# A row-sum kernel: late waits alone on SyncE's store and end, and the last row split into 576 and 448 columns

## The chip, the cores and the metric

The kernel runs on one core of one Trainium2 chip. The metric is the device time in microseconds (us) of one execution. The profile's span (first to last instruction) is about 1.8 us shorter than the device time, and times "at 157.9 us" count from the span's start.

Besides the profile's views, the argument uses the trace's records: the start of every instruction, also those of a sequencer alone, and every increment of a semaphore. A load "lands" here when its semaphore gets the last of its 16 increments. VectorE "signals" when the semaphore of its last operation is incremented. Both are recorded to the nanosecond.

Some terms: SyncE issues the loads and stores here, VectorE and ScalarE compute. A semaphore is a counter that an engine or a transfer raises and that others wait for. A sequencer handles an engine's instructions in order (SPq and DVEq in the views are those of SyncE and VectorE). A nop computes nothing, but can be given waits. The drain and the closing barrier are the program's last steps. "issue" in a chain of waits is time in which the engine waited for nothing that the profile shows.

## The reference

```python
# x: (32, 512, 1024) float32, multiplier: 0.5
def reference(x, multiplier):
    return (np.sum(x, axis=-1) * multiplier).astype(np.float32)
```

This is 16384 row sums over 67 MB of input. Each of the 128 partitions takes 128 rows.

## The kernel before

The kernel loads blocks of 16 rows per partition into three buffers, all from SyncE. In each of the first seven blocks VectorE sums eight rows and ScalarE sums eight. The results of these seven blocks, 112 rows per partition that lie together in memory (the pitch of 112 rows below), leave in one early store. The last block comes in five loads, so that little work is left when the last bytes land. Its last row is split into two pieces of columns, summed by two VectorE operations, of which the second starts from the first's sum.

```python
    own = rows - B                                   # 112 rows per partition
    out_rows = out_flat[0 : P * own].rearrange("(p c) -> p c", p=P)
    # ... pools, and the loop over the first seven blocks ...

    def dve_span(t, r, lo, hi, dst, start=0.0):
        mid = (lo + hi) // 2
        nc.vector.tensor_tensor_reduce(              # (left half + right half) * mul, summed into dst
            out=t[:, r, lo:mid], in0=t[:, r, lo:mid], in1=t[:, r, mid:hi],
            scale=mul, scalar=start, op0=ADD, op1=ADD, accum_out=dst,
        )

    cut = 640
    pieces = [(0, 8), (8, 13), (13, 15)]             # rows of the last block: three loads
    # ...
    for lo, hi in ((0, cut), (cut, D)):              # the last row: two loads
        loads.append(nc.sync.dma_start(
            out=t[:, B - 1, lo:hi], in_=x_last[:, B - 1, lo:hi]))
    nc.sync.dma_start(out=out_rows, in_=res[:, 0:own])           # the early store
    on_act = {4, 5, 6, 7, 11, 12, 14}
    # ... rows 0 to 14: ScalarE those of on_act, VectorE the others ...
    dve_span(t, B - 1, 0, cut, part)
    dve_span(t, B - 1, cut, D, res[:, rows - 1 : rows], start=part)

    seen = nc.sync.nop()                             # waits for the last 8 loads and ScalarE's last row
    # ... its dependencies ...
    store = nc.sync.dma_start(out=out_last, in_=res[:, own:])    # the last store
    # ... ordered behind seen ...
```

When an instruction has more waits than it can carry, the compiler puts semaphore instructions, which only wait, in front of it. In the records such an instruction carries at most two waits, and a store carries one. A nop with waits is not seen itself: its waits show up on semaphore instructions. How these waits are dealt out is what the change is about.

Of the kernel before, what the change touches and what calls it, by code (L numbers as in the profile page):

```python
# [1 line left out]

# [4 lines left out]


@with_exitstack
def kernel(  # L10
    ctx: ExitStack,
    tc: tile.TileContext,
    x: bass.AP,
    multiplier: float,
    out: bass.AP,
):








    nc = tc.nc
    P = nc.NUM_PARTITIONS
    fp32 = mybir.dt.float32
    ADD = mybir.AluOpType.add

    x_flat = x.flatten_outer_dims()  # L30
    N, D = x_flat.shape
    rows = N // P
    out_flat = out.rearrange("b s -> (b s)")
    mul = float(multiplier)

    B = 16
    n_blocks = rows // B
    assert N == P * rows and rows == n_blocks * B
    own = rows - B
    x_rows = x_flat[0 : P * own, :].rearrange("(p c) d -> p c d", p=P)  # L40
    x_last = x_flat[P * own : N, :].rearrange("(p c) d -> p c d", p=P)
    out_rows = out_flat[0 : P * own].rearrange("(p c) -> p c", p=P)
    out_last = out_flat[P * own : N].rearrange("(p c) -> p c", p=P)

    x_pool = ctx.enter_context(tc.tile_pool(name="x", bufs=3))
    res_pool = ctx.enter_context(tc.tile_pool(name="res", bufs=1))
    sums = res_pool.tile([P, rows], fp32, name="sums")
    res = res_pool.tile([P, rows], fp32, name="res")
    part = res_pool.tile([P, 1], fp32, name="part")

    loads = []
    acts = []

    def act_row(t, r, col):
        acts.append(nc.scalar.activation(  # L55
            out=t[:, r, :],
            in_=t[:, r, :],
            func=mybir.ActivationFunctionType.Copy,
            scale=mul,
            accum_out=res[:, col : col + 1],  # L60
        ))

    def dve_span(t, r, lo, hi, dst, start=0.0):
        mid = (lo + hi) // 2
        nc.vector.tensor_tensor_reduce(  # L65
            out=t[:, r, lo:mid],
            in0=t[:, r, lo:mid],
            in1=t[:, r, mid:hi],
            scale=mul,
            scalar=start,  # L70
            op0=ADD,
            op1=ADD,
            accum_out=dst,
        )

    for b in range(n_blocks - 1):
        c0 = b * B
        t = x_pool.tile([P, B, D], fp32, name="xb")
        loads.append(nc.sync.dma_start(out=t, in_=x_rows[:, c0 : c0 + B, :]))  # L79
        h = B // 2  # L80
        nc.vector.reduce_sum(  # L81
            out=sums[:, c0 : c0 + h], in_=t[:, 0:h, :], axis=mybir.AxisListType.X
        )
        nc.vector.tensor_single_scalar(  # L84
            out=res[:, c0 : c0 + h],
            in_=sums[:, c0 : c0 + h],
            scalar=mul,
            op=mybir.AluOpType.mult,
        )
        for r in range(h, B):  # L90
            act_row(t, r, c0 + r)

    c0 = (n_blocks - 1) * B
    t = x_pool.tile([P, B, D], fp32, name="xb")
    cut = 640
    pieces = [(0, 8), (8, 13), (13, 15)]
    for lo, hi in pieces:
        loads.append(
            nc.sync.dma_start(  # L99
                out=t[:, lo:hi, :], in_=x_last[:, lo:hi, :]  # L100
            )
        )
    for lo, hi in ((0, cut), (cut, D)):
        loads.append(
            nc.sync.dma_start(
                out=t[:, B - 1, lo:hi], in_=x_last[:, B - 1, lo:hi]
            )
        )
    nc.sync.dma_start(out=out_rows, in_=res[:, 0:own])
    on_act = {4, 5, 6, 7, 11, 12, 14}  # L110
    for r in range(B - 1):
        if r in on_act:
            act_row(t, r, c0 + r)
        else:
            dve_span(t, r, 0, D, res[:, c0 + r : c0 + r + 1])
    dve_span(t, B - 1, 0, cut, part)
    dve_span(t, B - 1, cut, D, res[:, rows - 1 : rows], start=part)



    seen = nc.sync.nop()
    for i in loads[-8:] + acts[-1:]:
        tc.add_manual_dep(
            seen.ins,
            i.ins.name,
            mybir.DependencyInfo(mybir.DependencyClass.Sync, mybir.DependencyReason.DATA),
            reason="ends seen early",
        )
    store = nc.sync.dma_start(out=out_last, in_=res[:, own:])
    tc.add_manual_dep(  # L130
        store.ins,
        seen.ins.name,
        mybir.DependencyInfo(mybir.DependencyClass.NoSync, mybir.DependencyReason.SCHED_ONLY),
        reason="in this order",
    )

    def start_loads_at_entry(nc_):



        entry, *rest = nc_.main_func.blocks
        is_sp = lambda i: i.engine == mybir.EngineType.SP
        is_load = lambda i: type(i).__name__ == "InstDMACopy"
        for block in rest:
            body = list(block.instructions)
            own = [i for i in body if is_sp(i)]
            if not any(is_load(i) for i in own):
                continue
            lead = []
            for i in own:  # L150
                if not is_load(i) or i.sync_info.on_wait:
                    break
                lead.append(i)
            names = {i.name for i in lead}
            block.instructions = [i for i in body if i.name not in names]
            head = list(entry.instructions)
            at = next(
                k for k, i in enumerate(head) if is_sp(i) and type(i).__name__ == "InstDrain"
            )
            entry.instructions = head[:at] + lead + head[at:]  # L160
            return

    nc.at_finalize(start_loads_at_entry)


# [1 line left out]
_INS = ['x', 'multiplier']  # L167
_OUTS = [((32, 512), 'float32')]

_NUMBERS = {'multiplier': 0.5}  # L170


# [26 lines left out]
```

## Time and profile before

| | before |
|---|---|
| time, median of 3 runs | 162.62 us (162.53 to 162.68) |
| span of the profile | 160.83 us |
| last load lands | 157.888 us |
| last landing to the end of the span | 2.938 us |
| VectorE, ScalarE busy | 42%, 42% |

The page of the kernel before, its span, its memory traffic and the chain that ended last, in shares of the span:

```profile
span 160.8 us, 236 instructions
...
HBM read 67.11 MB, written 0.07 MB: 418 GB/s over the span
## 4 chain that ended last, share of the span: by engine, by line
DMA 86%; DVE 11%; SPq 1%; issue 0%; DVEq 0%
```

Input DMA is 86% of the chain; the 11% of VectorE are reductions whose end frees a buffer for the next load. The change touches none of this. What it can reach is the tail after the last landing. The timeline from there on gives start, duration, engine, line, operation and operands:

```profile
157.47 0.49 DVE L65 CUSTOM_DVE_ANT_0 xb<-xb 128x320 f32<-128x320 f32 x1
157.58 0.18 ACT L55 ACTIVATION_READ_ACCUMULATOR xb<-xb 128x1 f32 x1
157.89 0.08 DVE L65 DVE_READ_ACCUMULATOR2_ANT part<- 128x1 f32 x1
158.02 0.42 DVE L65 CUSTOM_DVE_ANT_0 xb<-xb,part 128x192 f32<-128x192 f32 x1
158.37 0.08 DVE L65 DVE_READ_ACCUMULATOR2_ANT res<- 128x1 f32 x1
158.60 0.34 SPq L129 DMA_DIRECT2D out_dram<-res  x1
```

The two CUSTOM_DVE lines are the two spans of the last row (320 and 192 output columns, half of the columns read). The store goes out at 158.60. The end of the chain of waits, in order of time (start, us, what), shows what the profile holds responsible:

```profile
109.71 47.74 DMA xb<-in_x_dram
157.45 0.02 issue
157.47 0.49 DVE xb L65
157.96 0.02 DVE part L65
157.98 0.04 issue
158.02 0.42 DVE xb L65
```

By this view the second span (158.02) followed the first one's sum (`part`, 157.98).

The same stretch in the records of SyncE's sequencer (start in us, duration in ns, what the instruction waits for; these are not lines of a view):

```
157.947    28  semaphore instruction   ScalarE, load of the 640 columns
158.477    28  semaphore instruction   VectorE's last span, an old load
158.537    28  semaphore instruction   two old loads
158.604   344  store                   ScalarE
160.029    28  semaphore instruction   the store's landing (160.012), the early store
160.094     7  drain                   VectorE
160.152     7  drain                   closing barrier
```

VectorE signals at 158.461. A semaphore instruction with nothing new to wait for stands between that and the store, and the store itself carries a wait that was met at 157.78.

### The profile page before, as it was taken

The page shows a single profiled execution, that of the slowest core. Times are in us where ns is not written, and L with a number is a line of the kernel's source. Part 1 is how long each engine was busy: PE and PEld are TensorE (multiplying, and loading weights), DVE is VectorE, ACT ScalarE, POOL GpSimd, SP SyncE. Part 2 cuts the span into 40 slices and gives each one's busy share as a digit, 9 for nine tenths or more (in the row PEclk, how much of TensorE's full clock was granted, in tenths as well). Part 3 has the DMA queues.
Part 4 walks back from the last instruction along what each step waited for, and adds up shares of the span by engine and source line. Part 5 has one row for each costly group of instructions (what it writes and reads, how often), then busy time and mean ns, then how long its engine had stood idle before and what let it go on. Part 6 is the DMA issues. An engine that isn't in the chain of part 4 may idle for free.

```text
span 160.8 us, 236 instructions
## 1 busy us (share of the span) xinstructions
DVE 68.1 (42%) x34; ACT 67.9 (42%) x127; POOL 0.2 (0%) x4
## 2 busy tenths in 40 slices
DVE  0000059600794009920199002990049700597453
ACT  3000059500793009910099002980039700596952
POOL 0000000000000000000000000000000000000000
DMA  7996996996996996996996996996996996998990
GB/s 261 522 522 261 522 522 261 522 522 261 522 522 261 522 522 261 522 522 261 522 524 261 522 505 277 522 505 277 522 505 277 522 489 293 408 489 381 413 390 23
DMA packets 2017, 67.18 MB, mean 418 GB/s; under 512 B 480, under 2 KB 608, under 8 KB 736
## 3 DMA queue, kind: packets, MB, share of 16 engines
q1 hardware_dynamic: 2016, 67.18, 97.3%
q14 instruction: 1, 0.01, 0.0%
HBM read 67.11 MB, written 0.07 MB: 418 GB/s over the span
## 4 chain that ended last, share of the span: by engine, by line
DMA 86%; DVE 11%; SPq 1%; issue 0%; DVEq 0%
DMA xb<-in_x_dram 86%; DVE sums L81 11%; SPq L99 1%; DVE xb L65 1%; SPq L79 0%; DVE part L65 0%; DVEq L194 0%
## 5 line engine op out<-in xcount | busy, mean ns | idle before, releaser
L55 ACT ACTIVATE xb<-xb 128x1024 f32<-128x1024 f32 x63 | 65.6, 1042 | 88.2 <-DMA xb<-in_x_dram 88.2
L81 DVE TENSOR_REDUCE sums<-xb 128x8 f32<-128x8192 f32 x7 | 60.8, 8686 | 85.0 <-DMA xb<-in_x_dram 85.0
L55 ACT ACTIVATION_READ_ACCUMULATOR xb<-xb 128x1 f32 x63 | 11.8, 187 | 0.0
L65 DVE CUSTOM_DVE_ANT_0 xb<-xb 128x512 f32<-128x512 f32 (+1 forms) x9 | 5.6, 667 | 5.1 <-DMA xb<-in_x_dram 4.9
L55 ACT ACT_TABLE_LOAD x1 | 1.3, 1283 | 1.7 <-PEq L180 1.7
L84 DVE TENSOR_SCALAR res<-sums 128x8 f32<-128x8 f32 x7 | 1.2, 171 | 0.2
L65 DVE DVE_READ_ACCUMULATOR2_ANT res<- 128x1 f32 x9 | 0.7, 83 | 0.0
L65 DVE CUSTOM_DVE_ANT_0 xb<-xb,part 128x192 f32<-128x192 f32 x1 | 0.4, 419 | 0.1
L180 POOL MEMSET const-bfloat16-1.0<- 128x1 bf16 x1 | 0.1, 101 | 0.0
L180 POOL MEMSET const-uint8-127<- 128x1 uint8 x1 | 0.1, 101 | 0.0
L180 POOL MEMSET const-float32-0.0<- 128x1 f32 x1 | 0.1, 98 | 0.2 <-issue 0.2
L180 POOL MEMSET const-float32-1.0<- 128x1 f32 x1 | 0.1, 98 | 0.0
L65 DVE DVE_READ_ACCUMULATOR2_ANT part<- 128x1 f32 x1 | 0.1, 83 | 0.0
## 6 DMA issues: line engine op xcount, KB each, us to landing
xb<-in_x_dram SPq DMA_DIRECT2D x1, 4096.0 KB, 39.6
xb<-in_x_dram SPq DMA_DIRECT2D x1, 2560.0 KB, 45.4
xb<-in_x_dram SPq DMA_DIRECT2D x1, 1024.0 KB, 47.4
xb<-in_x_dram SPq DMA_DIRECT2D x1, 320.0 KB, 47.7
xb<-in_x_dram SPq DMA_DIRECT2D x1, 192.0 KB, 47.7
xb<-in_x_dram SPq DMA_DIRECT2D x7, 49.6
out_dram<-res SPq DMA_DIRECT2D x1, 56.0 KB, 10.8
out_dram<-res SPq DMA_DIRECT2D x1, 8.0 KB, 1.4
```

The source lines that it names most:

```text
L55: acts.append(nc.scalar.activation(out=t[:, r, :], in_=t[:, r, :], func=mybir.ActivationFunctionType.Copy, scale=mul, accum_out=res[:, col ...
L65: nc.vector.tensor_tensor_reduce(out=t[:, r, lo:mid], in0=t[:, r, lo:mid], in1=t[:, r, mid:hi], scale=mul, scalar=start, op0=ADD, op1=ADD, ...
L81: nc.vector.reduce_sum(out=sums[:, c0 : c0 + h], in_=t[:, 0:h, :], axis=mybir.AxisListType.X)
L84: nc.vector.tensor_single_scalar(out=res[:, c0 : c0 + h], in_=sums[:, c0 : c0 + h], scalar=mul, op=mybir.AluOpType.mult,)
L99: nc.sync.dma_start(out=t[:, lo:hi, :], in_=x_last[:, lo:hi, :])
L180: nc = _bacc.Bacc("TRN2", target_bir_lowering=False, num_devices=1)
```

## The change

The intent is that each late event is awaited by the instruction that needs it, with every older wait passed before. ScalarE's dependency is taken off the store, as the nop in front waits for it. A second nop behind the store waits for what the end would otherwise wait for, while the store is in flight. The last row is cut at 576 columns instead of 640. The 112-row pitch of the loads and the early store is in both kernels and is no edit here.

```diff
-    cut = 640
+    cut = 576
...
-    nc.sync.dma_start(out=out_rows, in_=res[:, 0:own])
+    early = nc.sync.dma_start(out=out_rows, in_=res[:, 0:own])
...
-    dve_span(t, B - 1, cut, D, res[:, rows - 1 : rows], start=part)
+    final = dve_span(t, B - 1, cut, D, res[:, rows - 1 : rows], start=part)
...
-    seen = nc.sync.nop()
-    (its dependencies, written out)
+    seen = nop_after(nc.sync, loads[-8:] + acts[-1:], [])
     store = nc.sync.dma_start(out=out_last, in_=res[:, own:])
     (ordered behind seen)
+    for a in acts[-len(on_act) :]:
+        tc.declare_no_dep(store.ins, a.ins.name, reason="waited for by the nop in front")
+    nop_after(nc.sync, [early, final], [store])
```

`nop_after(engine, waits_for, follows)` makes a nop that waits for the ends of the first list and is ordered behind the second.

## The prediction

> **What bounds the kernel.** The input's DMA. The page gives 67.11 MB read at 418 GB/s over a 160.8 us span, VectorE and ScalarE busy 42% each. The chain of waits is input DMA and the VectorE work that frees buffers (97%) up to the last landing near 157.9 us; the change touches none of that: the same bytes, issues and buffers. The pitch of 112 rows is already in the kernel before (the store and loads use it), so that part of the title is no edit here. What is left is the tail, 157.4 to 160.8 us.
>
> **The tail before** (timeline from 156 us, and the records of SyncE's sequencer and semaphores):
> - The last row's 640 columns land at 157.45, its 384 columns at 157.89. VectorE starts the first span at 157.470, its result is signalled at 157.98; the second span starts at 158.022 and signals at 158.461. So the first span's compute, not the last landing, releases the second: over 0.05 us after it could have.
> - SyncE then passes two semaphore instructions at the store's line (158.477 and 158.537) and issues the store at 158.604: 0.143 us from the signal to the issue. Only the first carries something late (VectorE's end); the rest had been true for long or since 157.95.
> - The store lands 1.41 us later, at 160.012. Then one semaphore instruction (160.029), a drain (160.094), and the closing barriers to 160.826.
>
> **What the change does.**
> 1. *Store.* ScalarE's dependency is dropped from the store, since the nop ahead waits for it. That should leave VectorE's end as the wait carried by the store itself, with the stale waits passed in front of it by about 158.1. Two semaphore instructions, 0.060 and 0.067 us in the trace, leave the path: estimate -0.12 us.
> 2. *End.* The early store's and VectorE's waits go into a nop behind the store, under its 1.41 us flight. The drain waits for the store alone: one semaphore instruction, 0.065 us, leaves: estimate -0.06 us.
> 3. *Split 576/448.* The first piece should land about 0.08 us earlier (the last engine's bytes, 20 KB before, took 0.85 us; 18 KB now), the last unchanged. VectorE's operation costs 492 ns for 320 output columns and 419 for 192, so 0.57 ns each: 288 cost 474, 224 cost 437. The first span is signalled at about 157.88, the second starts at the last landing, about 157.97, and signals at 158.42: estimate -0.04 us.
>
> All three lie in series on the path; together -0.22 us. The Trainium skill ("Perfetto Trace Analysis", Identifying Dependency Chains) says that several waits may put EventSemaphore instructions before an instruction; this trace agrees (two at the store, one at the end). The store's flight stays[...].
>
> **Prediction:** 162.41 us, 8 in 10 between 162.25 and 162.57. Chances: faster by over 2% 0.01, within 2% 0.98, slower 0.01.
>
> **What the profile should show.** The store issues under 0.05 us after VectorE's last signal, with no semaphore instruction between (step 1); the drain follows the store's landing directly, under 0.03 us (step 2); the second span starts within 0.1 us of the last landing and the first is done by then (step 3). Span near 160.6 us; loads unchanged up to 157.9.
>
> **What would make it wrong.** The compiler places waits its own way and leaves a stale one behind the late one; SyncE is still passing old waits when VectorE ends; the last landing moves by more than the 0.2 us sought (runs of the kernel before already spread 0.15 us); the second nop delays the end.

## The result

| | before | after |
|---|---|---|
| time, median of 6 runs each | 162.61 us (162.53 to 162.73) | 162.44 us (162.34 to 162.51) |
| last load lands (one profile) | 157.888 us | 157.827 us |
| last landing to the end of the span | 2.938 us | 2.791 us |

A ratio in this document is the mean time of one kernel's fast runs over that of the other's in the same rounds, so it is not quite the ratio of the medians. Here it is 0.9989, with a 95% interval from 0.9976 to 1.0002: the same within 2%, as forecast, and inside the range. The timed runs alone do not quite show a gain. The trace shows one in the tail, because the stretch after the last landing repeats to within a few ns.

The page of the kernel after, the lines that answer to those above:

```profile
span 160.6 us, 236 instructions
...
HBM read 67.11 MB, written 0.07 MB: 418 GB/s over the span
## 4 chain that ended last, share of the span: by engine, by line
DMA 86%; DVE 11%; SPq 1%; issue 0%; DVEq 0%
```

The timeline of the tail:

```profile
157.33 0.46 DVE L78 CUSTOM_DVE_ANT_0 xb<-xb 128x288 f32<-128x288 f32 x1
157.54 0.19 ACT L68 ACTIVATION_READ_ACCUMULATOR xb<-xb 128x1 f32 x1
157.72 0.08 DVE L78 DVE_READ_ACCUMULATOR2_ANT part<- 128x1 f32 x1
157.96 0.45 DVE L78 CUSTOM_DVE_ANT_0 xb<-xb,part 128x224 f32<-128x224 f32 x1 [0.16 <-DMA xb<-in_x_dram]
158.34 0.08 DVE L78 DVE_READ_ACCUMULATOR2_ANT res<- 128x1 f32 x1
158.45 0.34 SPq L136 DMA_DIRECT2D out_dram<-res  x1
```

The store now issues with no semaphore instruction between (158.45; VectorE's signal is at 158.432). But the first span's sum is there early (signalled at 157.812, before the landing at 157.827), and the second span still starts only at 157.961. The end of the chain of waits names what lies between:

```profile
110.15 47.68 DMA xb<-in_x_dram
157.83 0.03 issue
157.85 0.02 DVEq L78
157.88 0.09 issue
157.96 0.45 DVE xb L78
```

"DVEq L78" is a semaphore instruction on VectorE's own sequencer: the second span has two waits, carries the one for the first span's sum, and leaves the landing to the instruction in front. From the landing to the start it is 0.134 us. In the kernel before it is 158.022 - 157.888 = 0.134 us too. So the split did not move the start.

The tail, step by step, worked out as differences of the records. This table is the measuring tool of the rest:

| us | before | after | difference |
|---|---|---|---|
| last landing to start of the second span | 0.134 | 0.134 | 0 |
| start to VectorE's signal | 0.439 | 0.471 | +0.032 |
| signal to the store's issue | 0.143 | 0.017 | -0.126 |
| issue to the store's landing | 1.408 | 1.416 | +0.008 |
| landing to the closing barrier | 0.140 | 0.079 | -0.061 |
| barrier to the end | 0.674 | 0.674 | 0 |
| sum | 2.938 | 2.791 | -0.147 |

### The profile page after: what moved, and what is told of

It is laid out like the page before. It is cut to its first block, busy times and chain, and to the rows that moved or that the text cites. A ratio compares the mean times of both kernels' runs of the same rounds, so it can differ in the third digit from the quotient of the medians.

```text
span 160.6 us, 236 instructions
## 1 busy us (share of the span) xinstructions
DVE 68.1 (42%) x34; ACT 67.9 (42%) x127; POOL 0.2 (0%) x4
## 4 chain that ended last, share of the span: by engine, by line
DMA 86%; DVE 11%; SPq 1%; issue 0%; DVEq 0%
DMA xb<-in_x_dram 86%; DVE sums L94 11%; SPq L112 1%; DVE xb L78 0%; SPq L118 0%; SPq L92 0%; DVEq L78 0%; DVEq L199 0%
## 5 line engine op out<-in xcount | busy, mean ns | idle before, releaser
L78 DVE CUSTOM_DVE_ANT_0 xb<-xb 128x512 f32<-128x512 f32 (+1 forms) x9 | 5.6, 663 | 5.0 <-DMA xb<-in_x_dram 5.0
L78 DVE DVE_READ_ACCUMULATOR2_ANT res<- 128x1 f32 x9 | 0.7, 83 | 0.0
L78 DVE CUSTOM_DVE_ANT_0 xb<-xb,part 128x224 f32<-128x224 f32 x1 | 0.5, 452 | 0.2 <-DMA xb<-in_x_dram 0.2
L78 DVE DVE_READ_ACCUMULATOR2_ANT part<- 128x1 f32 x1 | 0.1, 84 | 0.0
```

The lines of the kernel that those rows point to most:

```text
L78: return nc.vector.tensor_tensor_reduce(out=t[:, r, lo:mid], in0=t[:, r, lo:mid], in1=t[:, r, mid:hi], scale=mul, scalar=start, op0=ADD, o ...
```

## The experiments

The new theory after reading the two traces: both wait edits do what was forecast; the split costs 0.03 us, because the landing's semaphore instruction sets the second span's start, and the second span got longer. Its rival for the split is the prediction's step 3 (the first span's sum sets the start). Its rival for the whole is that the measured 0.17 us is a matter of when the last landing came.

The last landing varied by 0.37 us over the 13 profiles (157.657 to 158.027), more than anything sought here. So single times decide little, and the verdicts below rest on the intervals behind the landing, with the times as a check. Each interval comes from one profile per run. The experiments ran on three chips, and where nothing was changed the intervals agree: from the landing to the start of a span with both waits 0.133 to 0.135 us in nine profiles, from the barrier to the end 0.673 to 0.675 in all 13.

### The parts, one at a time

`e1_split_only`, the kernel before with

```diff
-    cut = 640
+    cut = 576
```

> The kernel before with only the split 576/448. The prediction's step 3 (the end of the first span releases the second): the second span starts about 0.08 us after the last landing, instead of 0.134, and the time falls by about 0.04 us. New theory, from the trace after (the landing's semaphore instruction sets the start, and a column of VectorE output costs 1.04 ns, not 0.57): the start stays at 0.134 us after the landing, the signal comes 0.605 us after the landing instead of 0.573, and the time rises by about 0.03 us, which the runs may not resolve. Signal to store issue stays at 0.14 us under both.

`e2_waits_only`, the kernel after with

```diff
-    cut = 576
+    cut = 640
```

> The kernel after with the old split 640/384: the waits alone. Prediction: -0.18 us against before, so 0.04 slower than the whole change. New theory: last landing to signal 0.573 us, signal to store issue 0.017, store landing to closing barrier 0.079, in all 0.19 less than before from the last landing on, so 0.03 us better than the whole change. Rival, that the measured 0.17 us is mostly a matter of when the last landing came: the interval from last landing to end hardly moves.

`e3_store_only`, as e2 and

```diff
-    nop_after(nc.sync, [early, final], [store])
```

> Old split, ScalarE's dependency off the store, no nop at the end. Both theories: the store issues 0.017 us after VectorE's signal instead of 0.143 (-0.126), the end keeps its semaphore instruction (store landing to barrier 0.14 us). Time about -0.12 us against before. If the gain at the store came instead only together with the nop at the end, it stays at 0.14.

`e4_end_only`, as e2 and

```diff
-    for a in acts[-len(on_act) :]:
-        tc.declare_no_dep(store.ins, a.ins.name, reason="waited for by the nop in front")
```

> Old split, the store keeps ScalarE's dependency, the nop behind the store is there. Both theories: store issue stays 0.143 us after the signal, store landing to barrier 0.079 us instead of 0.140 (-0.061). Time about -0.06 us against before, at the limit of what the runs resolve.

Measured, 5 runs of each, against 9 of the kernel before on the same chip (median 162.54 us); intervals in us from one profile each:

| | median us | ratio to before (95%) | landing to start | start to signal | signal to store | store landing to barrier | last landing to end |
|---|---|---|---|---|---|---|---|
| before (first profile) | | | 0.134 | 0.439 | 0.143 | 0.140 | 2.938 |
| e1_split_only | 162.68 | 1.0007 (0.9994 to 1.0021) | 0.134 | 0.471 | 0.144 | 0.140 | 2.972 |
| e2_waits_only | 162.47 | 0.9990 (0.9978 to 1.0003) | 0.134 | 0.438 | 0.017 | 0.079 | 2.750 |
| e3_store_only | 162.44 | 0.9991 (0.9979 to 1.0004) | 0.134 | 0.439 | 0.017 | 0.140 | 2.814 |
| e4_end_only | 162.47 | 0.9997 (0.9985 to 1.0010) | 0.134 | 0.438 | 0.143 | 0.079 | 2.877 |

The store edit is worth 0.126 us and the end edit 0.061, each alone, and they add up: 2.938 - 2.750 = 0.188. The split alone lengthens the tail by 0.034 us. So step 3 has the wrong sign, and e2, the two wait edits without the split, has a tail 0.041 us shorter than the change as it was made (2.791; part of that is 0.008 of store flight, which varies). None of the four ratios is clear of 1 by itself; their order agrees with the intervals. The rival of the moving landing falls for the tail's part: e2's last landing came 0.055 us later than that of before, and its tail was still shorter.

The start stood at 0.134 us after the landing whether the first span's sum was signalled 0.016 us before the landing (e1) or 0.090 after it (e3). So it is not that sum that sets it.

### What a semaphore instruction behind the late one costs

`e8_two_behind`, the kernel after with `cut = 640` and two more nops in front of the store, so that VectorE's end is followed by older waits:

```diff
+    late = nop_after(nc.sync, [final], [seen])
+    stale = nop_after(nc.sync, [early] + loads[-4:-1], [late])
     store = nc.sync.dma_start(out=out_last, in_=res[:, own:])
```

> The kernel after with the old split 640/384, and between the nop and the store two more nops on SyncE: one that waits for VectorE's last span, then one that waits for the early store, which landed long before. VectorE's end is then waited for by a semaphore instruction with two stale ones behind it, ahead of the store. If each semaphore instruction after the late event costs its 0.06 us: signal to store issue 0.017 plus 3 times 0.063, about 0.20 us, more than in the kernel before (0.143). Rival, that the 0.126 us belongs to ScalarE's wait on the store and not to the number of instructions behind the late one: 0.02 us here, as ScalarE's wait is off the store.

Signal to store was 0.205 us. The records show the instruction that waits for VectorE at 158.375 (signal at 158.358), two with met waits at 158.436 and 158.496, and the store at 158.563, although ScalarE's wait is off the store. With none behind the signal it is 0.017 us, with two instructions on the path (before) 0.143, with three 0.205: about 0.063 us for each. The rival, that ScalarE's wait itself was the cost, falls. The time lost its gain too: 162.54 us (4 runs) against 162.59, ratio 1.0000 (0.9985 to 1.0016).

### What sets the second span's start and length

`e5_no_part` gives a wrong result (relative error 0.062): the kernel after, where the second span does not start from the first's sum, and row 0 of the last block starts from a tile of zeros.

```diff
+    zero = res_pool.tile([P, 1], fp32, name="zero")
+    nc.vector.memset(zero, 0.0)
...
-            dve_span(t, r, 0, D, res[:, c0 + r : c0 + r + 1])
+            start = zero if r == 0 else 0.0
+            dve_span(t, r, 0, D, res[:, c0 + r : c0 + r + 1], start=start)
...
-    final = dve_span(t, B - 1, cut, D, res[:, rows - 1 : rows], start=part)
+    final = dve_span(t, B - 1, cut, D, res[:, rows - 1 : rows])
```

> Wrong result on purpose (the first span of the last row is not added in): the kernel after, where the second span starts from 0.0 instead of the first's sum, so it waits for the landing alone, and where the first row of the last block takes its start from a tile of zeros. New theory: the second span carries the landing's wait itself and starts 0.023 us after the landing instead of 0.134; without the start operand its 224 columns take about 0.41 us to the signal instead of 0.471; row 0 with the zero tile takes about 0.05 us longer than row 1 with a constant. Prediction's reading (0.57 ns a column, the first span's end sets the start): the operand costs nothing, 0.47 us to the signal, and the start comes within 0.08 us of the landing.

The groups of VectorE instructions in its last 14 us, kept apart by shape (count, busy us, mean ns of one, idle before):

```profile
L80 DVE CUSTOM_DVE_ANT_0 xb<-xb 128x512 f32<-128x512 f32 x7 | 4.5, 688 | 4.0 <-DMA xb<-in_x_dram 4.0
L80 DVE CUSTOM_DVE_ANT_0 xb<-xb,zero 128x512 f32<-128x512 f32 x1 | 0.8, 750 | 0.9 <-DMA xb<-in_x_dram 0.9
L80 DVE CUSTOM_DVE_ANT_0 xb<-xb 128x288 f32<-128x288 f32 x1 | 0.5, 459 | 0.1
L80 DVE CUSTOM_DVE_ANT_0 xb<-xb 128x224 f32<-128x224 f32 x1 | 0.4, 391 | 0.1
```

The same operation with the operand in the kernel after (224 columns), and two spans of equal width in the run e6 below, one with and one without it:

```profile
L78 DVE CUSTOM_DVE_ANT_0 xb<-xb,part 128x224 f32<-128x224 f32 x1 | 0.5, 452 | 0.2 <-DMA xb<-in_x_dram 0.2
L78 DVE CUSTOM_DVE_ANT_0 xb<-xb,part 128x256 f32<-128x256 f32 x1 | 0.5, 486 | 0.2 <-DMA xb<-in_x_dram 0.2
L78 DVE CUSTOM_DVE_ANT_0 xb<-xb 128x256 f32<-128x256 f32 x1 | 0.4, 426 | 0.0
```

A start read from memory costs about 60 ns: 452 against 391 with 224 columns, 486 against 426 with 256. Row 0 of e5 took 750 ns, and the same row without the operand 691 to 694 in the other 12 profiles (the mean of 688 above is that of seven later rows). The Trainium skill ("VectorE: DVE Perf Modes", the section on the TRN2 errata) gives (N + 151)/0.96 ns for an fp32 tensor_tensor add, checked there at 512 and 2048 columns. An estimate from it is 691, 457 and 391 ns for 512, 288 and 224 columns, and the means of this trace agree to 3 ns where no start is read, though the operation here is a reduction. So a column costs about 1.04 ns (from the trace: (688 - 391)/(512 - 224) = 1.03), and the operand comes on top. The prediction took 492 ns (320 columns, no operand) and 419 ns (192, with it) as two points of one line and got 0.57 ns.

The chain of waits of e5 at the same place:

```profile
110.20 47.70 DMA xb<-in_x_dram
157.89 0.02 issue
157.92 0.39 DVE xb L80
```

With the landing as its only wait, the span starts 0.023 us after it, without the semaphore instruction: 0.111 us less. The Trainium skill ("Perfetto Trace Analysis", Per-engine timelines) says that a VectorE instruction is decoded and then waits in a hardware wait queue, while a sequencer-only one holds the sequencer until its waits are met. That would explain the 0.111 us, as the next instruction's way through the sequencer would then begin only after the landing; the runs show the cost, not the stages.

Last landing to end is 2.609 us, and the time is 162.19 us (4 runs; ratio 0.9977, 0.9964 to 0.9991). The tail is 0.182 us shorter than that of the kernel after: 0.111 at the start, 0.060 for the operand, and 0.010 of store flight, which varies. So the second span's dependency on the first costs 0.171 us. The next three runs therefore look for a right result that pays less.

`e6_nop_512`: the kernel after with a nop on VectorE that waits for the first span, and an even split.

```diff
-    cut = 576
+    cut = 512
...
-    dve_span(t, B - 1, 0, cut, part)
+    first = dve_span(t, B - 1, 0, cut, part)
+    part_seen = nop_after(nc.vector, [first], [first])
     final = dve_span(t, B - 1, cut, D, res[:, rows - 1 : rows], start=part)
+    (final ordered behind part_seen, and its own wait for first declared away)
```

> The kernel after with a nop on VectorE that waits for the first span, so that the second span carries only the landing's wait, and a split of 512/512 so that the first span is done early. New theory: the second starts 0.02 to 0.07 us after the last landing, takes 0.504 us to the signal (256 columns at 1.04 ns, plus the operand), so landing to signal 0.53 to 0.57 instead of 0.605 in the kernel after. Rival, that a VectorE start after a landing simply takes 0.13 us whatever carries the wait: landing to signal 0.64.

`e7_part_in_row`: the kernel after with `cut = 640`, where the second piece lands in a tile `tail` of 386 columns, the first span's sum goes (unscaled) into column 384, and column 385 is zero.

```diff
-    part = res_pool.tile([P, 1], fp32, name="part")
+    tail = res_pool.tile([P, 386], fp32, name="tail")
+    nc.vector.memset(tail[:, 385:386], 0.0)
...
+    (first span: scale=1.0, accum_out=tail[:, 384:385])
+    (second span: in0=tail[:, 0:193], in1=tail[:, 193:386], scale=mul, scalar=0.0)
```

> The kernel after with the old split 640/384, where the second piece lands in a tile of its own, and the first span's sum is written into a column behind it, with a column of zeros: the second span sums 386 columns and needs no start operand. It still waits for the landing and the first span. New theory: start 0.134 us after the landing as before, 193 columns take 0.385 us to the signal instead of 0.439, so landing to signal 0.52 (0.573 with the operand), time about 0.24 below before. If the operand costs nothing: 0.57.

`e9_row_nop_512`: both, with an even split (the tile has 514 columns, the second span 257 output columns).

> Both: the sum of the first span in the row's own columns, and the nop on VectorE, split 512/512. New theory: start 0.02 to 0.07 us after the last landing, 257 columns 0.45 us, so landing to signal 0.47 to 0.52 instead of 0.605, and time 0.26 to 0.30 below the kernel before (about 0.1 below the kernel after).

Measured, against 9 runs of before on the same chip (median 162.55 us):

| | median us | ratio to before (95%) | landing to start | start to signal | last landing to end |
|---|---|---|---|---|---|
| e6_nop_512 | 162.41 | 0.9988 (0.9975 to 1.0000) | 0.024 | 0.507 | 2.707 |
| e7_part_in_row | 162.33 | 0.9988 (0.9976 to 1.0001) | 0.133 | 0.381 | 2.691 |
| e9_row_nop_512 | 162.25 | 0.9980 (0.9966 to 0.9994) | 0.023 | 0.447 | 2.652 |

Each interval came as the new theory had it. e6 shows that a landing as the only wait starts the span in 0.024 us though it has the operand; e7 shows the operand gone with both waits still there. No run has the 512 cut without the nop, so e6 alone does not exclude that the earlier sum (0.165 us before the landing) brought the early start. Against that stands e5: its sum came 0.020 before the landing and its span started after 0.023, while e10 below, with the sum 0.040 before the landing but both waits, started after 0.135. e9's end of the chain is:

```profile
109.99 47.67 DMA tail<-in_x_dram
157.66 0.02 issue
157.68 0.43 DVE tail L142
```

One nuisance: one of e7's five runs took 162.74 us, which is why its ratio is no better than e6's although its median is.

### The better version beside the changed kernel

`e10_after_again` is the changed kernel unedited, `e11_row_nop_again` is e9 unedited, 5 runs each on one chip with 9 of before (median 162.59 us).

> The changed kernel unchanged, on the same chip as the next one. Last landing to end of span 2.79 us as in its first profile, of which landing to signal 0.605 us; time 0.1 to 0.2 us below before. The moment of the last landing may differ by 0.1 us or more.

> The same kernel as e9_row_nop_512, beside the changed kernel on one chip. Last landing to end of span 2.65 us as before, 0.14 less than the changed kernel, and a median about 0.1 to 0.2 us below it. If e9's advantage came from its early landings (157.66 us), the two medians are equal here.

| | median us | ratio to before (95%) | last landing | last landing to end |
|---|---|---|---|---|
| e10_after_again | 162.38 (162.34 to 162.45) | 0.9989 (0.9976 to 1.0001) | 157.797 | 2.787 |
| e11_row_nop_again | 162.29 (162.20 to 162.36) | 0.9982 (0.9970 to 0.9995) | 157.869 | 2.651 |

The tails repeat those of the first profiles to 0.004 us and 0.001 us. e11 landed 0.07 us later than e10 and its tail is still 0.136 us shorter, so e9's advantage did not come from its early landing. The difference of the medians is 0.09 us; the runs of the two overlap slightly. e9 is the best right version here: about 0.3 us below the kernel before, clear of noise in both batches, and still only 0.2%.

## Why the prediction was right or wrong

The forecast of 162.41 us met 162.44 us, and its range and its class held. Two of the three steps were right, and the third was wrong. The range is a weak test of the steps: e2 (162.47), e3 (162.44) and e4 (162.47) lie in it too.

1. *Store, -0.12 us: right.* It measured -0.126 (e3). It was read off the starts of SyncE's instructions in the trace before, and e8 showed that it is the number of instructions from the late event to the store that counts.
2. *End, -0.06 us: right.* It measured -0.061 (e4). The records after show the old waits at 158.839 and 158.893, under the store's flight, and the drain at 159.882, 0.017 us after the store's landing at 159.865.
3. *Split, -0.04 us: wrong in sign; +0.03.* The step that failed reads "So the first span's compute, not the last landing, releases the second". In the kernel before, both lay within 0.02 us: the first span's sum was signalled at 157.982, and an operation that carries the wait for a signal starts about 0.02 us after it (a reduction's signal at 147.019 to the next operation's start at 147.04), so 158.00; the landing with its semaphore instruction gave 158.022. The later of the two was the landing, so an earlier first span could gain nothing. The second term of the step was mis-sized as well: "0.57 ns each" for a column is 1.04 ns, because one of the two durations contained about 60 ns for the start operand. The longer second span then cost 0.032 us. With the old cut of 640 the first span's sum hides almost exactly behind the landing's semaphore instruction. The first half of the step did hold: the first piece landed 0.519 us before the last one instead of 0.441, and the first span's sum was there 0.015 us before the last landing. But the second span did not start "within 0.1 us of the last landing"; it took 0.134.

The sum of the three was forecast as -0.22 us; the tail shortened by 0.147. The profile's span nevertheless fell by about 0.21 us, because its last landing came 0.061 us earlier than that of the profile before. The four profiles with the 576 cut landed at 157.797 to 157.904, the six with the 640 cut at 157.785 to 158.014, so these 0.061 us cannot be put down to the change; as far as the runs show it was luck, and the forecast total was closer to the two profiles than its parts deserved. By the runs the whole change is 0.17 us by medians, with an interval of the ratio that still touches 1.

What stays open: why the last landing wanders by 0.37 us from run to run. Nothing in the tail can recover that.

## What to carry to other kernels

Where an instruction has several waits, it pays to know which one it carries itself and which go to instructions in front: let it carry the event that comes last, and have a nop pass the older ones earlier, on compute engines as on the issuing one. A chain of waits that names one releaser may hide a second one within a few hundredths of a microsecond; before tuning for the one, compute when the other would have let the work start. Before two durations are made into a slope, check that both operations have the same operands.

## What the Trainium skill lacked or had wrong

- "Perfetto Trace Analysis", Identifying Dependency Chains, says that semaphore instructions may be inserted for extra waits, but not what they cost. Here each one behind the late event cost 0.060 to 0.067 us on SyncE, and one that holds the late wait in front of a VectorE operation cost 0.111 us (0.134 from landing to start against 0.023).
- No page says which of several waits the instruction keeps. In these kernels the second span kept the wait for its own engine's earlier result and left the landing to the semaphore instruction; the store before kept the wait for ScalarE and left VectorE's.
- "VectorE: DVE Perf Modes", Scalar operands, describes a [P, 1] operand without a cost. Here a start read from memory added about 60 ns to an fp32 operation (486 against 426 ns, 452 against 391). The page's formula of (N + 151)/0.96 ns held within 4 ns, by the mean of each shape, for 193 to 512 columns without it.
- "DMA: Bandwidth & Descriptors", Anatomy of one DMA, gives about 2.0 us of fixed cost for the path issued from GpSimd. The 8 KB store from SyncE took 1.41 us from the start of its issue to its landing, 1.406 to 1.416 in all 13 profiles, so the page's figure should not be carried over to it.
